# A decoder trunk step on one core: the first norm's and MLP norm's factors from one ones-matmul on all partitions, and the second result of a pooling group three channel blocks behind the first

## The chip, the cores and the metric

The kernel runs on one core of a Trainium2 chip. The time is that of one execution on the device in microseconds, from launch to end; before the change three runs gave 1097.31, 1097.84 and 1098.05, median 1097.84. A profiled execution gives the span (first to last instruction), what each engine did and what it waited for. The engines are PE (TensorE: matmuls), DVE (VectorE), ACT (ScalarE), POOL (GpSimd) and SP (SyncE, which issues the DMAs). Each works through its own instructions in a fixed order, and semaphores hold one back until what it needs is there.

## What is computed

One layer on 256 prompt tokens and 8 x 4 sample tokens, 288 in all. Cut to what matters:

```python
def rmsnorm(x, g):
    y = xf * lax.rsqrt(jnp.mean(xf * xf, axis=-1, keepdims=True) + EPS)
    return (y * g.astype(jnp.float32)).astype(x.dtype)

h = rmsnorm(x, norm1_g)                                  # D_MODEL = 2048
proj = jnp.einsum("btd,de->bte", h, w_in) + b_in
a, gate, z = proj[..., :D_CONV], proj[..., D_CONV:2 * D_CONV], proj[..., 2 * D_CONV:]
u = a * jax.nn.sigmoid(gate)                             # depthwise causal conv of 31 taps,
c = jax.nn.silu(layernorm(depthwise_causal_conv(u_ext, conv_w, conv_b), ln_g, ln_b))
d = multiscale_pool(z_ext, pos0)                         # windows 2, 4, 8, 16; four groups of 256
p = jnp.einsum("btgc,gce->btge", d, pool_w).reshape(bsz, T, D_POOL) * pool_scale
mix = jnp.concatenate([c, p], axis=-1)
x = x + jnp.einsum("btm,md->btd", mix, w_out)
h2 = rmsnorm(x, norm2_g)
f = jnp.square(jax.nn.relu(jnp.einsum("btd,df->btf", h2, w_ff1)))   # D_FF = 8192
x = x + jnp.einsum("btf,fd->btd", f, w_ff2)
```

A last rmsnorm and the new states of conv and pooling follow. All data are float32.

## The kernel before

**Layout.** Channels lie on the 128 partitions and the 288 tokens (T) along the free axis; x is sixteen blocks of 128x288 (`xT`). A float32 product is made of three matmuls: each operand is split into a rounded part and the rest (`hh` and `hl`, `whi` and `wlo`), and `product` (lines 253 to 255) issues hi x hi, hi x lo and lo x hi into one PSUM bank. So a result block of 128 channels over 16 channel blocks is 48 matmuls of 128x288.

**Weights.** They arrive in raw tiles of 512 KB (four channel blocks of two results). ACT writes `whi` (line 246); POOL, or later DVE, writes `wlo` (line 247). Each has four buffers, so the cast of a tile waits until PE has done with the tile four before it. `ready` holds the weights of the next `gemm`.

**Gemms.** `gemm` (line 257) makes two result blocks at a time, in the banks `bk[0]` and `bk[1]`: for each channel block k the product of result 0, then that of result 1. Both end together. There are four banks for such results (`ac`), so a gemm needs the banks of the last but one to have been read.

**Order of the work.** The first two conv groups run while x arrives; then, by `SEQUENCE`, conv groups 2 to 6, pool groups 3, 2 and 1, mix 3, pool group 0, mix 2 and conv group 7, then mix 1 and 0; then w_out in two halves of eight gemms (the first over the pool results, `mixp`, the second over the conv results, `mixc`), x1 with the squares for MLP norm beside the second half, and the MLP in four chunks of 16 gemms. The names `ac1`, `ac2`, ... number the banks in that order: ac11 and ac12 are conv group 6, ac13 and ac14 pool group 3, ac17 and ac18 pool group 1, ac19 and ac20 mix 3, ac21 and ac22 pool group 0, ac43 and ac44 the last gemm of w_out's first half, ac45 to ac48 the first two of its second half.

**What sets the order on an engine.** The tile framework's scheduler does, with a simulated timeline: it takes the program's priorities, the sizes and the buffers, and fixes each engine's list before the run. `later` (the conv taps) lowers a priority. A small edit can so move instructions far from it.

**The norms.** The rms factor isn't applied to the activations ahead of a gemm; each result is multiplied by it when its bank is read (`rb` in lines 368, 369 and 414, `r2` in line 544). The squares are summed over blocks first. `token_sum` (line 221) then sums over partitions: three matmuls with the tokens as rows and a column of ones give 96 partitions x 3 columns. `rsqrt_rows` (line 223) makes the factor of these: sqrt on ACT, five small DVE operations (with one Newton step), and three matmuls with the identity (line 238) that spread the row over all partitions (`pr`). For the first norm DVE copies that to `rb` (line 356); for MLP norm ACT copies it to `r2` (line 541). The layer norm of the conv part (`norm_begin`, `norm_end`, within w_out's first half) and the last norm use `rsqrt_rows` too.

**A pool group** (line 404): a gemm over all 16 blocks; then per result DVE multiplies by `rb` (line 414), ACT adds the bias and writes prompt and samples to `z_all` (lines 415 and 416), DVE sums the windows, and ACT and DVE split the outcome for the mix.

Of the kernel before, what the change touches and what calls it, by code (L numbers as in the profile page):

```python
# [9 lines left out]
F32 = mybir.dt.float32  # L10
# [6 lines left out]
P = 128  # L17
# [63 lines left out]
def trunk_kernel(ctx: ExitStack, tc: tile.TileContext, io):  # L81
# [15 lines left out]
    def nm(s):  # L97
        seen[s] = seen.get(s, 0) + 1
        return f"{s}{seen[s]}"
# [122 lines left out]

    def rsqrt_rows(pt, scale, after=None):

        st = const.tile([TB, 2, 3], F32, name=nm("st"))
        s1, s2 = st[:, 0, :], st[:, 1, :]
        p, h = pt[:TB, 0:3], pt[:TB, 4:7]
        nc.scalar.activation(s1, p, AF.Sqrt, bias=eps[:TB, 0:1], scale=scale)
        if after is not None:
            load_table(after, s1[:, 0:1])  # L230
        nc.vector.tensor_scalar(h, p, scale / 2, EPS / 2, op0=ALU.mult, op1=ALU.add)
        nc.vector.reciprocal(s2, s1)
        nc.vector.tensor_tensor(h, h, s2, op=ALU.mult)
        nc.vector.scalar_tensor_tensor(out=s2, in0=s1, scalar=0.5, in1=h, op0=ALU.mult, op1=ALU.add)
        nc.vector.reciprocal(s1, s2)
        pr = ms("pr")
        for j in range(3):
            nc.tensor.matmul(pr[:, j * TB : (j + 1) * TB], s1[:, j : j + 1].to_broadcast([TB, P]), ident, start=True, stop=True)  # L238
        return pr

    def split(raw, eng, cuts=((0, 4),)):

# [11 lines left out]
        nc.tensor.matmul(b, wh, xl, start=False, stop=False)  # L254
        nc.tensor.matmul(b, wl, xh, start=False, stop=last)  # L255

    def gemm(banks, rhs, m_outer=False, hooks={}):

        n = len(rhs)
        get = ready.pop()  # L260
        order = [(k, m) for k in range(n) for m in range(len(banks))]
        if m_outer:
            order.sort(key=lambda km: km[1])
        for j, (k, m) in enumerate(order):
            hooks.get(j, bool)()
            product(banks[m], rhs[k], get(k, m), k == 0, k == n - 1)
        ready.extend(itertools.islice(weights, 1))
# [36 lines left out]

    hx = []
    first_banks = bank2() + [bank("cv", cvp, "cv") for _ in range(2)]
    total = ms("total", 8)

    def square(c):

# [8 lines left out]
    for c in range(8):  # L319
        pair = []  # L320
        hi = wspl.tile([P, 4, 256], F32R, name=nm("whi"), tag="whi")
        lo = wspl.tile([P, 4, 256], F32R, name=nm("wlo"), tag="wlo")
        views = [t[:].rearrange("p (b k) n -> p b k n", b=2) for t in (first_raw[c], hi, lo)]
        steps = ((0, 1), (1, 2)) if c < 2 else ((0, 2),)
        for k0, k1 in steps:
            for k in range(2 * c + k0, 2 * c + k1):
                hh, hl = act("hh"), act("hl")
                nc.scalar.activation(hh, xT[:, k, :], AF.Copy, scale=v("norm1_g", k))  # L328
                nc.vector.scalar_tensor_tensor(out=hl, in0=xT[:, k, :], scalar=v("norm1_g", k), in1=f32(hh), op0=ALU.mult, op1=ALU.subtract)
                pair.append((hh, hl))  # L330
            if len(steps) == 2:
                r, h, l = [t[:, :, k0, :] for t in views]
            else:
                r, h, l = first_raw[c], hi, lo
            nc.scalar.copy(h, r)  # L335
            nc.vector.tensor_tensor(l, r, h.bitcast(F32) if len(steps) == 2 else f32(hi), op=ALU.subtract)
            for w, x in ((hi, 0), (hi, 1), (lo, 0)):
                if c == 7 and w is lo:
                    token_sum(total, rows[0])
                for k in range(k0, k1):  # L340
                    for m in range(4):
                        nc.tensor.matmul(  # L342
                            first_banks[m][:, :T], lhs(w, k, m), pair[k][x],
                            start=c == 0 and k == 0 and w is hi and x == 0, stop=c == 7 and k == 1 and w is lo,
                        )
                if c == 7 and w is hi and x == 0:
                    square(6)
                    square(7)
                    rows = [row("tot")]
                    nc.vector.tensor_tensor(rows[0], squares[:, 0, 0], squares[:, 0, 1], op=ALU.add)  # L350
        hx += pair
        if 0 < c < 7:
            square(c - 1)
    ready.extend(itertools.islice(weights, 1))
    rb = row("rb")
    nc.vector.tensor_copy(rb, rsqrt_rows(total, 1.0 / D, AF.Sigmoid)[:, :T])
    nc.gpsimd.memset(z_all[:, :, 0:PH], 0.0)

    cs = {}
# [44 lines left out]
    def pool_group(g):  # L404

        bk = bank2()
        gemm(bk, hx)
        w = WINDOWS[g]
        for m in range(2):
            i = 2 * g + m  # L410
            z = z_all[:, i, :]
            zs = samples(z[:, ZO:ZL], ZS)
            p = bk[m][:, :T]
            nc.vector.tensor_tensor(p, p, rb, op=ALU.mult)
            nc.scalar.activation(z[:, PH:ZO], p[:, 0:SEQ], AF.Identity, bias=v("b_in", 16 + i))
            nc.scalar.activation(zs[:, :, PH:ZS], samples(p[:, SEQ:T], NS), AF.Identity, bias=v("b_in", 16 + i))  # L416
            b = ms("d")[:, :T]
            s, step, n = z, 1, w
            if w > 8:
                s, step, n = tmp("s", ZL, "s", 2), 4, w // 4  # L420
                nc.vector.tensor_reduce(s[:, 3:ZL], windows(z[:, 0 : ZL - 3], (1, ZL - 3), (1, 4)), axis=AX.X, op=ALU.add)
            at = PH - step * (n - 1)
            nc.vector.tensor_reduce(b[:, 0:SEQ], windows(s[:, at:], (1, SEQ), (step, n)), axis=AX.X, op=ALU.add)
            nc.vector.tensor_reduce(samples(b[:, SEQ:T], NS), windows(s[:, ZO + at :], (ZS, NB), (1, NS), (step, n)), axis=AX.X, op=ALU.add)
            nc.vector.tensor_tensor(b[:, 0 : w - 1], b[:, 0 : w - 1], rise[:, g, 0 : w - 1], op=ALU.mult)
            nc.vector.scalar_tensor_tensor(out=b[:, 0:SEQ], in0=b[:, 0:SEQ], scalar=1.0 / w, in1=z[:, PH:ZO], op0=ALU.mult, op1=ALU.subtract)
            bs = samples(b[:, SEQ:T], NS)
            nc.vector.scalar_tensor_tensor(out=bs, in0=bs, scalar=1.0 / w, in1=zs[:, :, PH:], op0=ALU.mult, op1=ALU.subtract)
            dh, dl = act("dh", tag="p", bufs=16), act("dl", tag="p", bufs=16)
            nc.scalar.copy(dh, b)  # L430
            nc.vector.tensor_tensor(dl, b, f32(dh), op=ALU.subtract)
            dd[i] = (dh, dl)
# [96 lines left out]
                nc.vector.tensor_tensor(ss2, ss2, q2, op=ALU.add)  # L529

    r2 = row("r2")
    pss = ms("pss", 8)
    ssf = row("ssf")
    pf = ms("pf", 8)
    for ch in range(DFF // FCH):
        fx = []
        for g in range(FCH // 256):
            bk = bank2()
            gemm(bk, x1, hooks={4: lambda: token_sum(pss, ss2)} if ch == 0 and g == 0 else {})
            if ch == 0 and g == 0:  # L540
                nc.scalar.copy(r2, rsqrt_rows(pss, 1.0 / D)[:, :T])
            for m in range(2):
                t = tmp("t")
                nc.vector.scalar_tensor_tensor(out=t, in0=bk[m][:, :T], scalar=0.0, in1=r2, op0=ALU.max, op1=ALU.mult)
# [97 lines left out]
```

## Time and profile before

| | |
|---|---|
| median of three runs | 1097.84 us |
| the profiled execution: time, span | 1098.09 us, 1096.3 us |
| granted TensorE clock, mean | 0.995 |
| gemm matmuls of the MLP: mean of one | 0.29 to 0.30 us, overlapping |
| weight loads of PE (PEld) | 1081.0 us, beside the matmuls |
| DMA | 187.04 MB, mean 171 GB/s |
| POOL, DVE busy from 30 to 130 us | 95.82, 88.61 of 100 us |
| ACT casts of weights, L246 | 330, 1.051 us each |

Busy time is the union of the instructions on an engine; matmuls are pipelined, so one lasts longer than the step to the next, and the step is what counts. A row of the view in order of time has start, duration, engine, line, operation, output and inputs with their shape, the number of records ("x2") and in square brackets how long the engine stood idle ahead of it and what released it. Line numbers are those of the kernel printed above; the changed kernel's are 15 to 17 higher behind the new functions.

### The profile page before, as it was taken

Reading aid. Unit: us, or ns where it says so; the run is one execution under the profiler, and the core shown is the slowest. Engines: PE = TensorE matmul, PEld = TensorE weight load, DVE = VectorE, ACT = ScalarE, POOL = GpSimd, SP = SyncE. Lnnn points to the kernel's source line nnn. Section 1 sums busy time; section 2 is a strip of 40 time slices with the busy share of each in tenths; the row PEclk is TensorE's granted clock in tenths of the full one; section 3 lists DMA queues with packets and bytes.
Section 4 is the critical chain, followed back from the end, with each engine's and each line's share of the span. In section 5 each row is a group of like instructions: output and inputs, shape, how many; then the busy total and the mean of one; then the engine's idle time right before and its main releaser. Section 6 shows DMA issues by size and latency. Waiting matters only on the chain.

```text
span 1096.3 us, 19737 instructions
## 1 busy us (share of the span) xinstructions
PE 1082.3 (99%) x8186; PEld 1081.0 (99%) x8186; DVE 631.0 (58%) x982; ACT 471.8 (43%) x650; POOL 162.8 (15%) x108
## 2 busy tenths in 40 slices
PE   9999999999999999999999999999999999999995
PEld 9999999999999999999999999999999999999995
DVE  7798989687554544444554444555544445554553
ACT  7544454476444433334443333444433334444441
POOL 0899878500000000000000000000000000000000
PEclk9999999999999999999999999999999999999998
DMA  9655568555555555555555555555555555555522
GB/s 335 221 184 167 173 162 236 161 165 171 158 170 161 170 168 165 168 171 160 170 170 164 167 173 162 167 172 169 161 171 162 166 172 167 162 171 164 166 94 87
DMA packets 56649, 187.04 MB, mean 171 GB/s; under 512 B 5872, under 2 KB 11504, under 8 KB 56560
## 3 DMA queue, kind: packets, MB, share of 16 engines
q1 hardware_dynamic: 56416, 185.74, 54.3%
q8 instruction: 64, 1.05, 0.4%
q14 instruction: 25, 0.20, 0.1%
q10 hardware_dynamic: 144, 0.05, 0.0%
HBM read 181.49 MB, written 4.28 MB: 169 GB/s over the span
## 4 chain that ended last, share of the span: by engine, by line
PE 98%; DVE 1%; ACT 0%; DMA 0%; SPq 0%; issue 0%; DVEq 0%
PE ac L253 32%; PE ac L254 32%; PE ac L255 31%; PE ac L342 1%; PE cv L342 1%; DMA xT<-in_xT 0%; DVE xT L582 0%; PE pr L238 0%; ACT hh L328 0%; ACT uz L312 0%; PE pf L221 0%; ACT whi L335 0%; DVEq L628 0%; PE m L253 0%; PE m L254 0%
## 5 line engine op out<-in xcount | busy, mean ns | idle before, releaser
L246 ACT CAST whi<-wr 128x1024 fp32r<-128x1024 f32 x330 | 346.6, 1051 | 583.9 <-PE ac L254 553.7
L247 DVE TENSOR_TENSOR wlo<-wr,whi 128x1024 fp32r<-128x1024 f32 x272 | 333.3, 1225 | 373.7 <-ACT whi L246 373.7
L253 PE MATMUL ac<-ah,whi 128*128 128x288 f32 x1024 | 303.2, 296 | 0.0
L253 PE MATMUL ac<-fh,whi 128*128 128x288 f32 x1024 | 303.1, 296 | 0.0
L254 PE MATMUL ac<-fl,whi 128*128 128x288 f32 x1024 | 301.7, 295 | 0.0
L254 PE MATMUL ac<-al,whi 128*128 128x288 f32 x1024 | 301.6, 295 | 0.0
L255 PE MATMUL ac<-fh,wlo 128*128 128x288 f32 x1024 | 299.8, 293 | 0.0
L255 PE MATMUL ac<-ah,wlo 128*128 128x288 f32 x1024 | 299.4, 292 | 0.0
L255 PEld LDWEIGHTS ac<-fh,wlo 128*128 128x128 f32 x1024 | 193.5, 189 | 0.0
L255 PEld LDWEIGHTS ac<-ah,wlo 128*128 128x128 f32 x1024 | 193.4, 189 | 0.0
L254 PEld LDWEIGHTS ac<-fl,whi 128*128 128x128 f32 x1024 | 193.0, 188 | 0.0
L254 PEld LDWEIGHTS ac<-al,whi 128*128 128x128 f32 x1024 | 192.6, 188 | 0.0
L253 PEld LDWEIGHTS ac<-ah,whi 128*128 128x128 f32 x1024 | 192.4, 188 | 0.0
L253 PEld LDWEIGHTS ac<-fh,whi 128*128 128x128 f32 x1024 | 192.3, 188 | 0.0
L247 POOL TENSOR_TENSOR wlo<-wr,whi 128x1024 fp32r<-128x1024 f32 x58 | 138.6, 2414 | 25.2 <-ACT whi L246 23.0
L395 DVE SCALAR_TENSOR_TENSOR pc<-uz,vec,pc 128x256 f32<-128x256 f32 x232 | 98.7, 482 | 6.8 <-ACT pc L384 4.8
L253 PE MATMUL ac<-hh,whi 128*128 128x288 f32 x320 | 93.7, 296 | 0.7 <-ACT uz L416 0.7
L254 PE MATMUL ac<-hl,whi 128*128 128x288 f32 x320 | 93.8, 297 | 0.0
L255 PE MATMUL ac<-hh,wlo 128*128 128x288 f32 x320 | 88.5, 295 | 0.0
L253 PEld LDWEIGHTS ac<-hh,whi 128*128 128x128 f32 x320 | 60.3, 188 | 1.0 <-ACT uz L416 1.0
L254 PEld LDWEIGHTS ac<-hl,whi 128*128 128x128 f32 x320 | 60.4, 189 | 0.0
L255 PEld LDWEIGHTS ac<-hh,wlo 128*128 128x128 f32 x320 | 58.5, 189 | 0.0
(153 smaller groups left out, 878.2 us busy)
## 6 DMA issues: line engine op xcount, KB each, us to landing
wr<-in_w SPq DMA_DIRECT2D x336, 512.0 KB, 3.8
out_u_out<-uz SPq DMA_DIRECT2D x1, 1208.0 KB, 9.5
xT<-in_xT SPq DMA_DIRECT2D x2, 576.0 KB, 7.9
out_yT<-xT SPq DMA_DIRECT2D x2, 576.0 KB, 2.9
uz<-in_hist_c SPq DMA_DIRECT2D x1, 1088.0 KB, 11.8
wr<-in_w SPq DMA_DIRECT2D x4, 256.0 KB, 5.1
xT<-in_xT SPq DMA_DIRECT2D x3, 288.0 KB, 5.8
out_z_out<-uz SPq DMA_DIRECT2D x1, 668.0 KB, 9.8
```

The source lines that it names most:

```text
L246: nc.scalar.copy(hi[:, a:b, :], raw[:, a:b, :])
L247: eng.tensor_tensor(lo[:, a:b, :], raw[:, a:b, :], hi[:, a:b, :].bitcast(F32), op=ALU.subtract)
L253: nc.tensor.matmul(b, wh, xh, start=first, stop=False)
L254: nc.tensor.matmul(b, wh, xl, start=False, stop=False)
L255: nc.tensor.matmul(b, wl, xh, start=False, stop=last)
L342: nc.tensor.matmul(first_banks[m][:, :T], lhs(w, k, m), pair[k][x], start=c == 0 and k == 0 and w is hi and x == 0, stop=c == 7 and k == 1 ...
L395: nc.vector.scalar_tensor_tensor(out=dst, in0=u_all[:, i, w : w + SEQ], scalar=cw[i][:, w : w + 1], in1=pc[i], op0=ALU.mult, op1=ALU.add)
```

## The change

- First norm and MLP norm: `wide_sum` multiplies the 128x128 matrix of ones with the 128x288 squares, so that every partition holds every token's sum; `rsqrt_wide` does the steps of `rsqrt_rows` on 128x288 and writes `rb` or `r2` with its last reciprocal. The three narrow sums, the three spreading matmuls and the copy go.
- `gemm` takes a `lag`; the pool groups call it with 3. Products are sorted by k + 3m: result 0 begins with three blocks of its own, then they alternate, and result 1 ends with three blocks of its own.
- `rsqrt_rows` (still used by the conv part's norm and the last norm) writes its last reciprocal to a column of its own instead of over the sqrt.

```diff
@@ -222,8 +222,8 @@
 
     def rsqrt_rows(pt, scale, after=None):
 
-        st = const.tile([TB, 2, 3], F32, name=nm("st"))
-        s1, s2 = st[:, 0, :], st[:, 1, :]
+        st = const.tile([TB, 3, 3], F32, name=nm("st"))
+        s1, s2, y = st[:, 0, :], st[:, 1, :], st[:, 2, :]
         p, h = pt[:TB, 0:3], pt[:TB, 4:7]
         nc.scalar.activation(s1, p, AF.Sqrt, bias=eps[:TB, 0:1], scale=scale)
         if after is not None:
@@ -232,11 +232,28 @@
         nc.vector.reciprocal(s2, s1)
         nc.vector.tensor_tensor(h, h, s2, op=ALU.mult)
         nc.vector.scalar_tensor_tensor(out=s2, in0=s1, scalar=0.5, in1=h, op0=ALU.mult, op1=ALU.add)
-        nc.vector.reciprocal(s1, s2)
+        nc.vector.reciprocal(y, s2)
         pr = ms("pr")
         for j in range(3):
-            nc.tensor.matmul(pr[:, j * TB : (j + 1) * TB], s1[:, j : j + 1].to_broadcast([TB, P]), ident, start=True, stop=True)
+            nc.tensor.matmul(pr[:, j * TB : (j + 1) * TB], y[:, j : j + 1].to_broadcast([TB, P]), ident, start=True, stop=True)
         return pr
+
+    def wide_sum(bank, t):
+
+        nc.tensor.matmul(bank[:, :T], ones, t, start=True, stop=True)
+
+    def rsqrt_wide(bank, out, scale, after=None):
+
+        s1, s2 = tmp("s"), tmp("s")
+        b = bank[:, :T]
+        nc.scalar.activation(s1, b, AF.Sqrt, bias=eps[:, 0:1], scale=scale)
+        if after is not None:
+            load_table(after, s1[:, 0:1])
+        nc.vector.tensor_scalar(b, b, scale / 2, EPS / 2, op0=ALU.mult, op1=ALU.add)
+        nc.vector.reciprocal(s2, s1)
+        nc.vector.tensor_tensor(b, b, s2, op=ALU.mult)
+        nc.vector.scalar_tensor_tensor(out=s2, in0=s1, scalar=0.5, in1=b, op0=ALU.mult, op1=ALU.add)
+        nc.vector.reciprocal(out, s2)
 
     def split(raw, eng, cuts=((0, 4),)):
 
@@ -254,13 +271,13 @@
         nc.tensor.matmul(b, wh, xl, start=False, stop=False)
         nc.tensor.matmul(b, wl, xh, start=False, stop=last)
 
-    def gemm(banks, rhs, m_outer=False, hooks={}):
+    def gemm(banks, rhs, m_outer=False, hooks={}, lag=0):
 
         n = len(rhs)
         get = ready.pop()
         order = [(k, m) for k in range(n) for m in range(len(banks))]
-        if m_outer:
-            order.sort(key=lambda km: km[1])
+        if m_outer or lag:
+            order.sort(key=lambda km: km[1] if m_outer else km[0] + lag * km[1])
         for j, (k, m) in enumerate(order):
             hooks.get(j, bool)()
             product(banks[m], rhs[k], get(k, m), k == 0, k == n - 1)
@@ -304,7 +321,7 @@
 
     hx = []
     first_banks = bank2() + [bank("cv", cvp, "cv") for _ in range(2)]
-    total = ms("total", 8)
+    total = ms("total")
 
     def square(c):
 
@@ -336,7 +353,7 @@
             nc.vector.tensor_tensor(l, r, h.bitcast(F32) if len(steps) == 2 else f32(hi), op=ALU.subtract)
             for w, x in ((hi, 0), (hi, 1), (lo, 0)):
                 if c == 7 and w is lo:
-                    token_sum(total, rows[0])
+                    wide_sum(total, rows[0])
                 for k in range(k0, k1):
                     for m in range(4):
                         nc.tensor.matmul(
@@ -353,7 +370,7 @@
             square(c - 1)
     ready.extend(itertools.islice(weights, 1))
     rb = row("rb")
-    nc.vector.tensor_copy(rb, rsqrt_rows(total, 1.0 / D, AF.Sigmoid)[:, :T])
+    rsqrt_wide(total, rb, 1.0 / D, AF.Sigmoid)
     nc.gpsimd.memset(z_all[:, :, 0:PH], 0.0)
 
     cs = {}
@@ -404,7 +421,7 @@
     def pool_group(g):
 
         bk = bank2()
-        gemm(bk, hx)
+        gemm(bk, hx, lag=3)
         w = WINDOWS[g]
         for m in range(2):
             i = 2 * g + m
@@ -529,16 +546,16 @@
                 nc.vector.tensor_tensor(ss2, ss2, q2, op=ALU.add)
 
     r2 = row("r2")
-    pss = ms("pss", 8)
+    pss = ms("pss")
     ssf = row("ssf")
     pf = ms("pf", 8)
     for ch in range(DFF // FCH):
         fx = []
         for g in range(FCH // 256):
             bk = bank2()
-            gemm(bk, x1, hooks={4: lambda: token_sum(pss, ss2)} if ch == 0 and g == 0 else {})
+            gemm(bk, x1, hooks={4: lambda: wide_sum(pss, ss2)} if ch == 0 and g == 0 else {})
             if ch == 0 and g == 0:
-                nc.scalar.copy(r2, rsqrt_rows(pss, 1.0 / D)[:, :T])
+                rsqrt_wide(pss, r2, 1.0 / D)
             for m in range(2):
                 t = tmp("t")
                 nc.vector.scalar_tensor_tensor(out=t, in0=bk[m][:, :T], scalar=0.0, in1=r2, op0=ALU.max, op1=ALU.mult)
```

The edits move instructions elsewhere too. The lists below are each engine's instructions in program order (line, operation, output and inputs with the tiles' numbers, shape of the output; the second number in a name is internal).

ACT where pool group 1 (ac17 and ac18) and mix 3 (ac19 and ac20) end; `uz` is the state buffer that holds z, `ph` a split mix result, `dh` a split pooling result. Before:

```order
L443 ACTIVATE ph1_1917<-ac19_1879,vec_85 128x288
L415 ACTIVATE uz_87<-ac17_1743,vec_85 128x256
L416 ACTIVATE uz_87<-ac17_1743,vec_85 128x8x4
L443 ACTIVATE ph2_1921<-ac20_1880,vec_85 128x288
L415 ACTIVATE uz_87<-ac18_1744,vec_85 128x256
L416 ACTIVATE uz_87<-ac18_1744,vec_85 128x8x4
```

and now, where ac17's two instructions stand ahead of `ph1`:

```order
L263 CAST whi44_1895<-wr44_1889 128x1024
L432 ACTIVATE uz_87<-ac17_1737,vec_85 128x256
L433 ACTIVATE uz_87<-ac17_1737,vec_85 128x8x4
L460 ACTIVATE ph1_1911<-ac19_1873,vec_85 128x288
L460 ACTIVATE ph2_1915<-ac20_1874,vec_85 128x288
L432 ACTIVATE uz_87<-ac18_1738,vec_85 128x256
L433 ACTIVATE uz_87<-ac18_1738,vec_85 128x8x4
```

The reads of ac17 moved ahead of `ph1`, and the cast of whi44 is still the row before them.

PE around the end of pool group 3's predecessor: `ac11` and `ac12` are conv group 6, `ac13` is the first result of pool group 3. The last matmul on `whi25` and the first on `whi29`, which takes its buffer, now (the row with `hl4_231,whi25` is the last of its tile):

```order
L270 MATMUL ac12_1272<-hh4_230,whi25_1169 128x288
L271 MATMUL ac12_1272<-hl4_231,whi25_1169 128x288
L272 MATMUL ac12_1272<-hh4_230,wlo25_1170 128x288
L270 MATMUL ac11_1271<-hh5_251,whi26_1173 128x288
L271 MATMUL ac11_1271<-hl5_252,whi26_1173 128x288
L270 MATMUL ac12_1272<-hh5_251,whi26_1173 128x288
L271 MATMUL ac12_1272<-hl5_252,whi26_1173 128x288
L270 MATMUL ac13_1437<-hh1_174,whi29_1373 128x288
L271 MATMUL ac13_1437<-hl1_175,whi29_1373 128x288
L272 MATMUL ac11_1271<-hh5_251,wlo26_1174 128x288
L272 MATMUL ac12_1272<-hh5_251,wlo26_1174 128x288
```

Before, the same first matmul stood here, thirty rows behind the last one on `whi25`:

```order
L254 MATMUL ac12_1278<-hl9_328,whi27_1187 128x288
L253 MATMUL ac13_1443<-hh1_174,whi29_1379 128x288
L254 MATMUL ac13_1443<-hl1_175,whi29_1379 128x288
L253 MATMUL ac14_1444<-hh1_174,whi29_1379 128x288
L254 MATMUL ac14_1444<-hl1_175,whi29_1379 128x288
L255 MATMUL ac11_1277<-hh9_327,wlo27_1188 128x288
L255 MATMUL ac12_1278<-hh9_327,wlo27_1188 128x288
```

So the first two matmuls of pool group 3 have moved 24 rows forward, into conv group 6's second tile, and ac14's remain where tile 27 begins.

DVE where w_out's second half begins: `n` is a normalized conv block, `cc` its silu, `mh` and `ml` the split of it that the second half multiplies, and the additions to `xT` read the banks ac43 and ac44 of the first half's last gemm. Before:

```order
L492 TENSOR_TENSOR n1_2665<-c1_536,pr2_2661 128x288
L247 TENSOR_TENSOR wlo69_2977<-wr69_2972,whi69_2976 128x1024
L492 TENSOR_TENSOR n2_2673<-c2_539,pr2_2661 128x288
L497 TENSOR_TENSOR ml1_2668<-cc1_2669,mh1_2667 128x288
L492 TENSOR_TENSOR n3_2681<-c3_868,pr2_2661 128x288
L504 TENSOR_TENSOR xT_86<-xT_86,ac43_2857 128x288
L492 TENSOR_TENSOR n4_2689<-c4_871,pr2_2661 128x288
L504 TENSOR_TENSOR xT_86<-xT_86,ac44_2858 128x288
L497 TENSOR_TENSOR ml2_2676<-cc2_2677,mh2_2675 128x288
```

and now:

```order
L509 TENSOR_TENSOR n2_2667<-c2_533,pr1_2655 128x288
L509 TENSOR_TENSOR n3_2675<-c3_862,pr1_2655 128x288
L264 TENSOR_TENSOR wlo69_2971<-wr69_2966,whi69_2970 128x1024
L509 TENSOR_TENSOR n4_2683<-c4_865,pr1_2655 128x288
L521 TENSOR_TENSOR xT_86<-xT_86,ac43_2851 128x288
L509 TENSOR_TENSOR n5_2691<-c5_1195,pr1_2655 128x288
L514 TENSOR_TENSOR ml1_2662<-cc1_2663,mh1_2661 128x288
L521 TENSOR_TENSOR xT_86<-xT_86,ac44_2852 128x288
L509 TENSOR_TENSOR n6_2699<-c6_1198,pr1_2655 128x288
L264 TENSOR_TENSOR wlo70_2975<-wr70_2968,whi70_2974 128x1024
L514 TENSOR_TENSOR ml2_2670<-cc2_2671,mh2_2669 128x288
```

`ml1` came behind `n2` and ahead of ac43's addition; now it comes behind that addition and `n5`, and `ml2` behind the weight split `wlo70`. On ACT, likewise, `mh1` came behind the first `cc` and now comes behind the third, and the cast of whi70 ahead of `mh2`.

## The prediction

> **What bounds the kernel now.** I read the page first, then the list of what PE waits for, then the order in time around each place that the change touches.
>
> ```profile
> PE 1082.3 (99%) x8186; PEld 1081.0 (99%) x8186; DVE 631.0 (58%) x982; ACT 471.8 (43%) x650; POOL 162.8 (15%) x108
> PE 98%; DVE 1%; ACT 0%; DMA 0%; SPq 0%; issue 0%; DVEq 0%
> ```
>
> PE is busy for 99% of the span and holds 98% of the chain that ended last. So time is won in two ways only: fewer PE instructions, or fewer moments in which PE stands still. Inside the run there is one such moment:
>
> ```profile
> PE ac L253 <- ACT uz L416: 0.7, 1, 0.7
> ```
>
> The profiled execution took 1098.09 us, its span is 1096.3, so 1.8 lie around it; the median of the three timed runs, 1097.84, is 0.25 below it. The sum is made against 1098.09 and 0.25 is taken off at the end. A measurement of this kernel tells about 0.2%, 2.2 us, from no change.
>
> **Part 1: the two norms on PE.** In time order on PE (start, duration, line, operation); "x6" are six records of three matmuls:
>
> ```profile
> 27.59 0.59 PE L221 MATMUL total<-ones,tot 128*96 128x1 f32 x6
> 28.04 0.52 PE L342 MATMUL ac<-hl,whi 128*128 128x288 f32 x2
> 28.39 0.43 PE L342 MATMUL cv<-hl,whi 128*128 128x288 f32 x2
> ...
> 32.90 0.81 PE L238 MATMUL pr<-ident,st 96*128 96x96 f32 x6
> ...
> 33.70 0.30 PE L254 MATMUL ac<-hl,whi 128*128 128x288 f32 x1
> ...
> 278.75 0.59 PE L221 MATMUL pss<-ones,ss 128*96 128x1 f32 x6
> ...
> 279.42 0.29 PE L254 MATMUL ac<-al,whi 128*128 128x288 f32 x1
> ...
> 285.26 0.81 PE L238 MATMUL pr<-ident,st 96*128 96x96 f32 x6
> ...
> 286.07 0.30 PE L254 MATMUL ac<-al,whi 128*128 128x288 f32 x1
> ```
>
> Durations overlap, so I count starts. Gemm matmuls start 0.132 us apart (twelve starts, 135.78 to 137.24 below, are 11 steps in 1.46). The first token sum with two matmuls takes 28.39 - 27.59 = 0.80, of which two steps are the matmuls': it displaces 0.54. The first pr with one matmul takes 0.80: it displaces 0.67. For MLP norm it is 0.67 - 0.13 = 0.54 and 0.81 - 0.13 = 0.68. All four go: 2.43. What comes is two matmuls of a 128x128 f32 matrix by 128x288 f32. The kernel has that form once already, the mean of the conv groups:
>
> ```profile
> 201.47 0.65 PE L473 MATMUL pmean<-sum_c,avg 128*128 128x288 f32 x2
> 201.74 0.51 PE L255 MATMUL ac<-ph,wlo 128*128 128x288 f32 x1
> 202.09 0.29 PE L253 MATMUL ac<-ph,whi 128*128 128x288 f32 x1
> ```
>
> That is 202.09 - 201.47 - 0.13 = 0.49 each, 0.98 for both. **Part 1 gives 2.43 - 0.98 = 1.45 us less**, straight on the bound.
>
> **The rest of the norms.** Five DVE operations of 96x3 become five of 128x288, and a copy goes (DVE for the first norm, ACT for MLP norm).
>
> ```profile
> 33.74 0.46 DVE L356 COPY rb<-pr 128x288 f32<-128x288 f32 x1 [3.54 <-PE pr L238]
> ...
> 281.12 0.17 DVE L231 TENSOR_SCALAR pss<-pss 96x3 f32<-96x3 f32 x1 [0.35 <-ACT st L228]
> 281.19 0.16 DVE L232 RECIPROCAL st<-st 96x3 f32<-96x3 f32 x1
> ```
>
> A 128x288 operation takes 0.46. No row has a reciprocal that wide. At three elements it costs what a TENSOR_SCALAR does, so the near end is 0.46; a difference of 0.02 us would be seen there, which is 0.007 an element, so 0.46 + 288 x 0.007 = 2.5 us is an end that these rows bear; scaled by elements alone, 0.16 x 96 = 15 us, it is the far one. I take 0.46, since the 0.16 is a fixed cost by its neighbour: TENSOR_SCALAR's 0.17 scaled so would be 16 us as well, and a wide two-operand operation takes 0.46. [...]
>
> It hides behind PE: rb was ready at 33.74 + 0.46 = 34.2. With 2.5 a reciprocal, the chain from 28.1 is sqrt 0.5, three operations 1.4 and two reciprocals 5.0, so 35.0; DVE stood idle there (3.54 before the copy). PE first needs a bank that waits for rb 133 instructions behind the sum, 17.6 us, at about 45. For MLP norm it is 142 instructions, 18.7 us. Queued behind a slow reciprocal on DVE stand weight splits of L247, whose results are used some 70 matmuls (9 us) later. So: nothing. The reused st slot that rsqrt_rows gives up takes a wait from the group norm's last reciprocal, which lies ahead of an idle DVE: nothing either.
>
> **Part 2: pool groups.** The lag changes no instruction count; it moves when two results end and when two pairs of weight tiles are first and last used. Three places answer, and the queues.
>
> *Start of pool group 0 (the one stall).* PE, ACT and DVE in time order:
>
> ```profile
> 135.52 0.29 PE L254 MATMUL ac<-hl,whi 128*128 128x288 f32 x1
> ...
> 135.78 0.29 PE L253 MATMUL ac<-dh,whi 128*128 128x288 f32 x1
> ...
> 137.24 0.29 PE L255 MATMUL ac<-dh,wlo 128*128 128x288 f32 x1
> 138.28 0.40 PE L253 MATMUL ac<-hh,whi 128*128 128x288 f32 x1 [0.74 <-ACT uz L416]
> 138.51 0.30 PE L254 MATMUL ac<-hl,whi 128*128 128x288 f32 x1
> ```
> ```profile
> 135.90 1.05 ACT L246 CAST whi<-wr 128x1024 fp32r<-128x1024 f32 x1 [2.13 <-PE ac L254]
> 137.18 0.50 ACT L443 ACTIVATE ph<-ac,vec 128x288 fp32r<-128x288 f32 x1 [0.23 <-PE ac L255]
> 137.57 0.47 ACT L415 ACTIVATE uz<-ac,vec 128x256 f32<-128x256 f32 x1
> 137.93 0.29 ACT L416 ACTIVATE uz<-ac,vec 128x32 f32<-128x32 f32 x1
> ```
> ```profile
> 135.86 0.44 DVE L414 TENSOR_TENSOR ac<-ac,rb 128x288 f32<-128x288 f32 x1
> ```
>
> PE loses 138.28 - 137.24 - 0.13 = 0.91 and another 0.10 in a slow first step (0.23 for 0.13): 1.01. DVE was done with ac17 at 136.30; ACT read it only at 137.57, because the cast (held until 0.38 behind the start of a matmul on the old tile, 135.52) and the mix result ph1 stood ahead. Now L432 and L433 of ac17 stand ahead of ph1. With E the start of mix 3: cast from E + 0.12 to 1.17, L432 at 1.17, L433 from 1.53 (0.36 behind, as 137.57 to 137.93) to 1.82, PE on again 0.06 later, at 1.88, against 1.59 when its twelve matmuls are through. **0.30 + 0.10 stay of 1.01: 0.6 less**; the ends are 1.01 less and nothing.
>
> *Start of pool group 3.* The order shows that its first matmul, ac13 with whi29, was drawn forward into the end of conv group 6: it now stands six matmuls behind the last one that reads whi25, whose buffer the cast of whi29 takes; before it were thirty. By the rows above a cast starts 0.38 behind the start of the matmul that frees its buffer, takes 1.05 and lets PE go 0.06 later: 1.49, against 6 x 0.132 = 0.79. Before, thirty matmuls (4.0 us) covered it. **A new stall, 0.70 + 0.10: 0.8 more.** Ends: nothing (if something else had set that cast's time) and 1.3 (if the 0.5 us activation ahead of it is late as well).
>
> *Queues.* SP's transfers keep their order; on POOL one split trades places with an L388 product in the first conv groups and near 160 us a sum of L400 goes ahead of one split. A split of the weights on POOL takes 2.41 us:
>
> ```profile
> L247 POOL TENSOR_TENSOR wlo<-wr,whi 128x1024 fp32r<-128x1024 f32 x58 | 138.6, 2414 | 25.2 <-ACT whi L246 23.0
> ```
>
> Two splits are first used 24 matmuls, 3.2 us, apart, so with a sum of some 0.8 between them the second is still in time: nothing.
>
> *Start of w_out's second half.* The scheduler has also reordered DVE and ACT where the first conv result meets w_out:
>
> ```profile
> 217.51 0.81 PE L238 MATMUL pr<-ident,st 96*128 96x96 f32 x6
> ...
> 221.20 0.43 PE L253 MATMUL ac<-mh,whi 128*128 128x288 f32 x2
> 221.47 0.30 PE L254 MATMUL ac<-ml,whi 128*128 128x288 f32 x1
> ```
> ```profile
> 218.73 1.22 DVE L247 TENSOR_TENSOR wlo<-wr,whi 128x1024 fp32r<-128x1024 f32 x1
> ...
> 220.23 0.45 DVE L497 TENSOR_TENSOR ml<-cc,mh 128x288 fp32r<-128x288 f32 x1
> ...
> 221.01 0.45 DVE L504 TENSOR_TENSOR xT<-xT,ac 128x288 f32<-128x288 f32 x1
> ```
> ```profile
> 218.84 0.63 ACT L495 ACTIVATE cc<-n,vec 128x288 f32<-128x288 f32 x1 [0.31 <-DVE n L492]
> 219.50 0.43 ACT L496 CAST mh<-cc 128x288 fp32r<-128x288 f32 x1
> ```
>
> Before, ml1 was done at 220.68 and PE took it at 221.47, 0.8 us to spare. Now ml1 stands behind the x addition of ac43 and n5 on DVE. That addition waits for a matmul four ahead of the second half's first (G): released at G - 0.53 + 0.38 = G - 0.15, then n5 and ml1 one step of 0.37 each behind it, ml1 from G + 0.59 to 1.04, PE on at 1.10. The three first matmuls that need only mh1 last to G + 0.5 (the third waits 0.1 for the addition): a hole of 0.6. Twelve matmuls later it wants ml2, which now stands behind ac44's addition, n6 and a weight split of 1.13: done at G + 3.27, wanted at about G + 2.9: 0.4. With slow first steps of 0.10 each: **about 1.25 more**. The ends are nothing (as before) and 2.0 (two more DVE steps of 0.37 ahead of ml1).
>
> **Sum:** -1.45 - 0.6 + 0.8 + 1.25 = 0.0. So 1098.1 on the profiled scale, **1097.8 us** on that of the median: the gain is real, and is given back.
>
> **The rivals.**
> - *Only one of the two new stalls forms:* -0.8 or -1.25, so 1097.0 or 1096.6. For it: both rest on times worked out, not seen. 0.14.
> - *Neither forms:* 1097.84 - 1.45 - 0.6 = 1095.8, and 1095.4 if pool group 0's stall goes too. For it: the same two places held in the profile of before, and DVE and ACT are 58% and 43% busy. Against it: an engine's order is fixed, and a matmul six places behind the release of a 1.05 us cast can't be fed in 0.79. 0.16.
> - *The lag leaves pool 0's stall as it is*, since something else releases it: 0.6 more, 1098.4. 0.05.
> - *The wide reciprocal becomes the bound, and it is slower than before.* Place: DVE, between the sqrt and the first use of the factor. The point where two reciprocals outlast the cover is, in the first norm, (17.6 - 0.5 - 1.9 and the four evictions ahead of the bank, 1.5, so 13.7) / 2 = 6.9 us each; behind that each microsecond counts twice. At 8 us it is 2.3 there and, with the MLP norm's 1 us more of cover, 1.2 there: +3.5, 1101.3; at the far end of 15 us some 30 more. Against it: the 0.16 beside 0.17. 0.06.
> - *The TensorE clock falls in the stalls.* At the program's start eight matmuls took 6.97 - 4.92 = 2.05 us, twice the usual step; a stall in w_out's second half followed by 3.8 us at that half speed would cost 1.9, two of them 3.8: 1101.6. The row behind the 0.91 us stall of before has a granted clock of 1.00 (seventh figure, ahead of the DMA share). [...] 0.02.
>
> ```profile
> 4.92 0.83 PE L342 MATMUL ac<-hh,whi 128*128 128x288 f32 x2
> ...
> 6.97 0.42 PE L342 MATMUL ac<-hh,wlo 128*128 128x288 f32 x2
> ```
> ```profile
> 138.20:142.00 3.80, 3.72 (x27) 3.73 (x28) 3.80 (x13) 1.36 (x6) 1.21 (x1) 1.00 0.64 201
> ```
>
> **How the numbers follow.** The forecast has 0.57. It, the single stall and the unchanged pool 0 lie within 0.2% (0.76); so does a third of "neither" (0.05): same 0.81. Two thirds of "neither", with pool 0's stall gone as well or part 1 a little better, fall below 1095.65: faster 0.11. The last two make slower 0.08. The bounds of the terms give -1.45 - 1.01 = -2.5 and -1.45 + 1.3 + 2.0 = +1.9, so 1095.4 to 1099.7; the slower two stay outside.
>
> **What would show it.** PE's waits in the changed profile should list ACT whi under the gemm (0.7, at pool group 3's start), DVE ml (two, 1.0 together), and ACT uz at 0.3 in place of 0.7; the two sums should displace 0.49 each and nothing of pr be left but the group norm's and the last norm's. rb's reciprocal should end before 36 us. Were the ACT whi and DVE ml waits missing, the gain of 2 us would stand and I am wrong on the low side; a wait for rb or r2 in PE's list would be the reciprocal.

## The result, and the profile after

The changed kernel takes 1103.51 us (median of 6 runs, 1102.94 to 1104.51) against 1097.41 for the kernel before beside it (6 runs, 1096.82 to 1098.05): a ratio of 1.0053, 95% interval 1.0043 to 1.0063. It is slower, and outside the predicted range. The profiled span is 1101.9 us against 1096.3.

The page of the changed kernel: busy time by engine, and the chain that ended last.

```profile
PE 1086.6 (99%) x8166; PEld 1084.3 (98%) x8166; DVE 639.6 (58%) x981; ACT 472.0 (43%) x649; POOL 162.9 (15%) x108
```
```profile
PE 98%; DVE 1%; DMA 0%; ACT 0%; SPq 0%; issue 0%; DVEq 0%; ACTq 0%
```

PE has 20 instructions fewer and is busy for 4.3 us longer. What it waited for (total, times, longest, in us):

```profile
PE ac L359 <- ACT whi L352: 1.5, 2, 1.3
PE pr L238 <- DVE st L235: 1.2, 1, 1.2
PE warm L209 <- DVE ones L195: 1.1, 1, 1.1
PE pf L221 <- ACT q L582: 1.0, 1, 1.0
PE ac L271 <- DVE ml L514: 0.6, 2, 0.3
PE ac L270 <- ACT whi L263: 0.5, 1, 0.5
```

The last two rows are the new stalls, at w_out's second half (DVE ml, two of them) and at pool group 3 (ACT whi); the wait for uz has sunk out of the list. The first is in the loop over the arriving input, at the program's start. It was 0.4 before and lies between 0.2 and 1.6 in the kernels below; the first norm's sum starts between 27.2 and 28.1 us in all of them, against 27.59 before, so less than half a microsecond comes of it. The predicted places, in time order on PE in the changed kernel:

```profile
27.66 0.65 PE L243 MATMUL total<-tot,ones 128*128 128x288 f32 x2
27.93 0.65 PE L359 MATMUL ac<-hl,whi 128*128 128x288 f32 x2
28.41 0.29 PE L359 MATMUL cv<-hl,whi 128*128 128x288 f32 x1
...
87.75 0.30 PE L271 MATMUL ac<-hl,whi 128*128 128x288 f32 x1
88.57 0.40 PE L270 MATMUL ac<-hh,whi 128*128 128x288 f32 x1 [0.52 <-ACT whi L263]
88.81 0.29 PE L271 MATMUL ac<-hl,whi 128*128 128x288 f32 x1
...
137.61 0.29 PE L272 MATMUL ac<-dh,wlo 128*128 128x288 f32 x1
137.91 0.40 PE L270 MATMUL ac<-hh,whi 128*128 128x288 f32 x1
138.15 0.29 PE L271 MATMUL ac<-hl,whi 128*128 128x288 f32 x1
...
220.81 0.71 PE L270 MATMUL ac<-mh,whi 128*128 128x288 f32 x3
221.85 0.40 PE L271 MATMUL ac<-ml,whi 128*128 128x288 f32 x1 [0.33 <-DVE ml L514]
222.09 0.29 PE L272 MATMUL ac<-mh,wlo 128*128 128x288 f32 x1
...
223.15 0.69 PE L270 MATMUL ac<-mh,whi 128*128 128x288 f32 x4
224.09 0.40 PE L271 MATMUL ac<-ml,whi 128*128 128x288 f32 x1 [0.24 <-DVE ml L514]
224.32 0.29 PE L272 MATMUL ac<-mh,wlo 128*128 128x288 f32 x1
...
279.56 0.65 PE L243 MATMUL pss<-ss,ones 128*128 128x288 f32 x2
279.83 0.51 PE L270 MATMUL ac<-ah,whi 128*128 128x288 f32 x1
280.17 0.29 PE L271 MATMUL ac<-al,whi 128*128 128x288 f32 x1
```

Read by starts, less 0.13 us for each matmul that belongs there: the sums displace 0.49 and 0.48; pool group 3 stalls for 0.69 and a slow first step of 0.11; pool group 0 for 0.17 and 0.11 (1.01 before); w_out's second half for 0.64 + 0.11 and 0.41 + 0.10. Beside the prediction's terms:

```
term                       predicted   measured
both norms on PE             -1.45       -1.46
pool group 0's stall         -0.6        -0.73
pool group 3's new stall     +0.8        +0.80
w_out's two new stalls       +1.25       +1.26
sum                           0.0        -0.13
span                          0.0        +5.6
```

Every term of the sum came out, and 5.7 us came from somewhere else. Two pairs of rows show where: the MLP norm's sum pss (quoted above and in the prediction), and the program's last token sum (before, then after).

```profile
1083.49 0.67 PE L221 MATMUL pf<-ones,q 128*96 128x1 f32 x6 [1.02 <-ACT q L565]
```
```profile
1089.07 0.67 PE L221 MATMUL pf<-ones,q 128*96 128x1 f32 x6 [1.02 <-ACT q L582]
```

Up to pss the changed kernel takes 279.56 - 278.75 = 0.81 more, where the terms ahead of it give 0.6 (-0.72 for the first norm, -0.73 + 0.80 + 1.26). From pss to pf it takes 809.51 against 804.74: 4.77 more, where the list of its instructions holds 0.74 less (the MLP norm's own part). So **the MLP is 5.5 us slower on an unchanged list**: but for the norm's own, the same 6144 matmuls in the same order. It isn't a stall: the only row of PE's waits that lies there is the 1.02 ahead of pf, in both. Eight gemms in the middle of the MLP, 768 matmuls from the first on x1's first block to the first on fx, before and after:

```profile
475.74 0.30 PE L253 MATMUL ac<-ah,whi 128*128 128x288 f32 x1
...
576.70 0.30 PE L253 MATMUL ac<-fh,whi 128*128 128x288 f32 x1
```
```profile
476.82 0.30 PE L270 MATMUL ac<-ah,whi 128*128 128x288 f32 x1
...
578.58 0.30 PE L270 MATMUL ac<-fh,whi 128*128 128x288 f32 x1
```

100.96 us are 131.5 ns a matmul, 101.76 are 132.5. Cut into eighths of 768 matmuls, and without the first and the last, which hold the norm's sum and that of the last norm, the MLP runs at 131.4 to 131.9 before and at 132.5 after. 6144 matmuls at 0.9 ns are 5.5 us. Neither the clock (seventh figure) nor the DMA (eighth and ninth: share, GB/s) differs between the two (windows view, before and after):

```profile
500.00:600.00 100.00, 100.00 (x763) 100.00 (x762) 50.22 (x63) 42.98 (x60) 0.00 (x0) 1.00 0.54 166
```
```profile
500.00:600.00 100.00, 100.00 (x757) 100.00 (x756) 51.20 (x62) 42.10 (x60) 0.00 (x0) 1.00 0.53 167
```

The start times of successive matmuls show what differs: both kernels repeat a pattern of steps, and not the same one. From the 19th gemm of the MLP, in ns (the changed kernel, and the same kernel with one more matmul, the last experiment below, which steps much as the kernel before does):

```
changed kernel         137 126 132 133 133 132 | 138 126 131 134 132 133 | 137 126 132 133 132 133
with one more matmul   133 130 126 131 134 132 131 132 131 | 133 130 126 131 134 132 131 132 131
```

The steps repeat with a period of six, at a mean of 132.2, against a period of nine, at 131.1. The last quarter of that gemm follows another pattern in both, with some longer steps; with it the means are 132.5 and 131.4. I call them the slow and the fast rhythm.

### The profile page after: what moved, and what is told of

It is laid out like the page before. It is cut to its first block, busy times and chain, and to the rows that moved or that the text cites. A ratio compares the mean times of both kernels' runs of the same rounds, so it can differ in the third digit from the quotient of the medians.

```text
span 1101.9 us, 19685 instructions
## 1 busy us (share of the span) xinstructions
PE 1086.6 (99%) x8166; PEld 1084.3 (98%) x8166; DVE 639.6 (58%) x981; ACT 472.0 (43%) x649; POOL 162.9 (15%) x108
## 4 chain that ended last, share of the span: by engine, by line
PE 98%; DVE 1%; DMA 0%; ACT 0%; SPq 0%; issue 0%; DVEq 0%; ACTq 0%
PE ac L270 32%; PE ac L272 32%; PE ac L271 32%; PE ac L359 1%; PE cv L359 1%; DMA xT<-in_xT 0%; DVE xT L599 0%; PE pr L238 0%; DVE wlo L264 0%; PE pf L221 0%; ACT whi L263 0%; ACT hh L345 0%; SPq L171 0%; SPq L164 0%; DVE n L509 0%
```

## The experiments

Times are medians beside the kernel before on the same chip, ratios have their 95% intervals. "MLP" is from the start of pss to the start of the pf group behind q, "ahead" is what lies before; ns is the step over the eight gemms above.

**Which part of the change?** Each part was put into the kernel before by itself, and the changed kernel was run without the lag. In question were (A) the buffers, which take turns in another order in the MLP when something ahead of it has moved, (B) a rhythm of PE that the MLP norm's small matmuls shift, (C) the pool groups' order with the lag. The diffs are cut to the added lines that matter; `wide_sum` and `rsqrt_wide` are those of the change, and `rsqrt_rows` keeps its old slot wherever a part stands alone.

First norm alone:

```diff
+    total = ms("total")
+                    wide_sum(total, rows[0])
+    rsqrt_wide(total, rb, 1.0 / D, AF.Sigmoid)
```


> Only the first norm is made wide; MLP norm, the pool groups and the st slot are as before. The profile of the change shows that its extra time lies in the MLP: 131.4 to 132.0 ns from one matmul to the next before, 132.5 after, over 6144 matmuls (5.5 us), on the same list of instructions. Theory A: the buffers decide (this kernel's weight tiles and PSUM banks take turns as in the changed kernel), so the MLP runs at 132.5 ns here too and the time is 1103.5. Theory B: a rhythm of PE that the small matmuls of MLP norm's old form shift early in the MLP (they are still here), so 131.4 to 132.0 ns and 1098.0. Both: the stalls at pool group 3's start (0.7) and w_out's second half (0.6 and 0.4) are here as well, since this kernel's lists have them too.

MLP norm alone:

```diff
+    pss = ms("pss")
+            gemm(bk, x1, hooks={4: lambda: wide_sum(pss, ss2)} if ch == 0 and g == 0 else {})
+                rsqrt_wide(pss, r2, 1.0 / D)
```


> Only MLP norm is made wide; the rest is as before. The buffers take turns as before. Theory A (the buffers decide): the MLP at 131.4 to 132.0 ns a step, 1096.7 us. Theory B (the removed small matmuls decide): 132.5 ns, 1102.2 us. Both: no new stall, since the lists of pool group 3 and of w_out's second half are as before.

Lag alone:

```diff
+        if m_outer or lag:
+            order.sort(key=lambda km: km[1] if m_outer else km[0] + lag * km[1])
+        gemm(bk, hx, lag=3)
```


> Only the lag of 3 in the pool groups; both norms and the st slot as before. Its buffers take turns as in the changed kernel, its first matmul of pool group 3 stands 30 behind (as before), its w_out second half has the changed order. Theory A: the MLP at 132.5 ns, 1103.4 us. Theory B: 131.4 to 132.0 ns, 1097.9 us. Both: the stall of pool group 0 shrinks to 0.2 to 0.3, no stall at pool group 3, 0.6 and 0.4 at w_out's second half.

The changed kernel without the lag:

```diff
-        gemm(bk, hx, lag=3)
+        gemm(bk, hx)
```


> Both norms wide and the st slot, without the lag. Theories A and B: the MLP at 132.5 ns, 1102.7 us. If the lag were needed for the slow MLP (theory C: it is the pool groups' own order that does it), 131.4 to 132.0 ns and 1097.2 us. The stalls are those of the changed kernel in all cases, by the order of the lists.

And the MLP norm and the lag without the first norm (the diffs of the second and third together, the old slot too):

> MLP norm wide and the lag, the first norm as before. Its lists have the changed order at w_out's second half (stalls of 0.6 and 0.4) and pool group 0 (0.3 in place of 1.0), not at pool group 3. By the sum 1097.4 - 0.7 - 0.7 + 1.2 = 1097.2 us with the MLP at 131.4 to 132.0 ns, 1102.5 us with it at 132.5. If what comes ahead of the MLP (the w_out part of the list) sets the rhythm, it is 132.5 as in the three other kernels with that part; if MLP norm's form sets it, 131.4 to 132.0 as in the kernel with MLP norm alone.

```
in the kernel                      us       ratio                     ahead    MLP      ns
nothing (before)                                                     278.75   804.74   131.5
first norm                       1104.35   1.0059 [1.0044, 1.0074]   279.75   810.23   132.5
MLP norm                         1097.06   0.9992 [0.9983, 1.0002]   278.65   803.87   131.5
lag                              1103.41   1.0050 [1.0033, 1.0067]   279.04   810.24   132.5
both norms                       1103.17   1.0050 [1.0035, 1.0065]   279.47   809.51   132.5
MLP norm and lag                 1096.80   0.9992 [0.9983, 1.0001]   278.98   803.67   131.4
all three (the change)           1103.51   1.0053 [1.0043, 1.0063]   279.56   809.51   132.5
```

MLP takes one of two values, some 804 to 805 or 810 us, and what the kernels do in it differs by some 0.7 only. The first norm alone brings the slow one, the lag alone too, the MLP norm doesn't: as theory A had it in the first four, where B and C each missed. But the lag with the MLP norm is fast. So the lag has no price of its own in the MLP, and it adds nothing to the two norms (the last row against that of both); nor does the MLP norm's form decide, since the changed kernel has it and is slow. The first norm is in slow kernels each time in this table; that it can be fast as well, the last experiment shows.

These runs also say where the moves ahead of the MLP come from. PE's waits in the kernel with the first norm alone, and in the one with the lag alone:

```profile
PE ac L271 <- DVE ml L514: 0.6, 2, 0.3
PE ac L270 <- ACT whi L263: 0.5, 1, 0.5
```
```profile
PE ac L254 <- DVE ml L497: 0.6, 2, 0.3
```

The first norm alone has the new stalls at both places (and pool group 0's has shrunk to 0.18); the lag alone has w_out's and no stall at pool group 3.

**Is it which buffer is read when?** Behind the MLP norm the lists of both kernels are the same but for the buffers, which take turns in another order: the two banks of a gemm's results (2, 1 and 3, 0 where they were 2, 3 and 0, 1), and the four buffers each of whi (2 3 1 0 for 3 2 1 0) and wlo (2 1 3 0). Fixed turns for the banks:

```diff
+    turn = itertools.count()
-        return [bank("ac") for _ in range(2)]
+        return [acc.tile([P, 512], F32, name=nm("ac"), tag=f"ac{(0, 1, 2, 3)[next(turn) % 4]}", bufs=1) for _ in range(2)]
```


> The changed kernel with the four result banks taken in a fixed turn, so a gemm has banks 0 and 1 or 2 and 3 (in the changed kernel it has 2 and 1 or 3 and 0; before the change 2 and 3 or 0 and 1). The weight tiles take turns as in the changed kernel (whi buffers 2 3 1 0, wlo 2 1 3 0). Theory A1, the pairs of banks decide: the MLP at 131.4 to 132.0 ns a step and 1098.0 us. Theories A2 and A3 (below): 132.5 ns and 1103.5 us.

1105.53, 1.0070 [1.0055, 1.0085], MLP 809.50, 132.5 ns: A1 fails. The fixed turn also brought a new stall of 1.6 us ahead of the MLP, up to 153.7 us.

The turn of the weights can be changed by one matmul that reads a weight tile again, late enough to hold its buffer past its turn; the result goes to a bank that nobody reads. In the diffs, cut to the place from here on, the numbers in braces count from 0: the gemm (or chunk and gemm), and the product ahead of which the matmul stands; `once_more(k, part)` reads the tile of channel block k, part 0 being whi and 1 wlo:

```diff
+    def once_more(k, part):
+        spare = ms("spare")
+        nc.tensor.matmul(spare[:, :T], keep[0](k, 0)[part], x1[0][0], start=True, stop=True)
...
+ {3: {24: lambda: once_more(4, 0)}}.get(g, {}) if ch == 0 else {}
```


> The changed kernel with one matmul more, without a use for its result, in the fourth gemm of the MLP: it reads a whi tile once more behind the last use of the next tile, so that two whi buffers come free in the other order and take turns 2 1 3 0 from there on, as wlo does; no other instruction moves. Theory A2, what decides is whether whi and wlo take turns in the same order: 131.4 to 132.0 ns from the sixth MLP gemm on, 1098.6 us. Theory A1 (banks) and A3 (whi's turn in descending order, 3 2 1 0): 132.5 ns and 1103.7 us.

1098.19, 1.0003 [0.9994, 1.0013], MLP 804.12, 131.4 ns from the next gemm on. Taken by itself, that speaks for the turns, as theory A2 has it. The next two put whi alone, and then both, to the turn of the kernel before:

```diff
+ {3: {16: lambda: once_more(0, 0)}}
```


> As the run with whi's turn like wlo's, but the extra matmul stands eight products earlier, so that whi takes turns 3 2 1 0 (its order before the change) and wlo stays at 2 1 3 0. Theory A3: 131.4 to 132.0 ns, 1098.6 us. Theory A2: 132.5 ns or slower, since the orders still differ, 1103.7 us. Theory A1: 132.5 ns, 1103.7 us.

```diff
+ {3: {16: lambda: once_more(0, 0), 24: lambda: once_more(4, 1)}, 4: {16: lambda: once_more(0, 1)}}
```


> Three extra matmuls in the fourth and fifth MLP gemm, so that whi and wlo both take turns 3 2 1 0 from there, as before the change; banks as in the changed kernel. Theories A2 and A3: 131.4 to 132.0 ns, 1098.9 us. Theory A1: 132.5 ns, 1104.0 us.

1103.50, 1.0052 [1.0037, 1.0067], and 1104.04, 1.0055 [1.0038, 1.0072]; both 132.5 ns. With the weights' turns those of before the MLP is still slow, so A2 and A3 fail. Two theories were left: M, that the whole assignment of buffers decides, and L, that it tells nothing and that small disturbances put PE into one rhythm or the other. Two runs bear on M: all turns, banks too, as before in the changed kernel, and the kernel before with one whi turn changed by such a matmul.

```diff
+ {3: {16: lambda: once_more(0, 0), 24: lambda: once_more(4, 1)}, 4: {16: lambda: once_more(0, 1)}}
+        return [acc.tile([P, 512], F32, name=nm("ac"), tag=f"ac{(0, 1, 2, 3)[next(turn) % 4]}", bufs=1) for _ in range(2)]
```


> The changed kernel with whi and wlo both at turns 3 2 1 0 from the fifth MLP gemm on and the banks in order (0 and 1, 2 and 3): all of the assignment of before the change. Theory M: 131.4 to 132.0 ns from there on; with the 1.8 us stall that the fixed banks alone brought near 152 us, 1100.7 us. Theory L: the assignment tells nothing; 132.5 ns as in the run with both orders descending (1105.9 us) or 131.4 to 132.0.

```diff
+ {3: {24: lambda: once_more(4, 0)}}
```


> The kernel before the change with the one extra matmul of the run that gave whi wlo's turn, at the same place; here it makes the turns differ (whi 3 1 2 0, wlo 3 2 1 0). Theory M as far as it says that differing turns are slow: 132.5 ns from the sixth MLP gemm on, 1102.8 us. Theory L: the turns tell nothing; the extra matmul alone does or doesn't disturb the rhythm (1097.9 or 1102.8), and it then does the same in the run with the eleven at this first place.

1105.79, 1.0074 [1.0059, 1.0089], 132.5 ns; and 1098.03, 1.0003 [0.9994, 1.0013], 131.5 ns. M misses both. The buffers of before don't bring its pace, and another turn doesn't take it away. Two kernels of the table above show the same from the other side: in the programs as built, the one with the first norm alone and the one with MLP norm and lag read and write the same addresses in each of the MLP's matmuls behind the norm's sum, and the first is slow, the second fast.

**Is it the disturbance itself?** Extra matmuls that read a tile still in use, so that no turn moves, at places spread over the MLP, in the changed kernel and in the kernel before. Of eleven places two name a product beyond the gemm's 32 and add nothing.

```diff
+ {(0, 3): {24: lambda: once_more(12, 0)}, (0, 6): {8: lambda: once_more(4, 0)}, (1, 1): {16: lambda: once_more(8, 0)}, ...
```


> The changed kernel with eleven single matmuls more in the MLP, without a use for their results, at different places of its gemms (two or three in each quarter of the MLP, two gemms apart); each reads a tile that is in use anyway, so that no buffer's turn and no other instruction moves. The runs so far leave two theories. Theory M: the whole assignment of buffers decides (whi, wlo and banks together; no one of them alone). Then the MLP stays at 132.5 ns a step between all eleven, 1105 us. Theory L: on one list and one assignment PE has two rhythms, each of which keeps itself up, and small disturbances decide which one it falls into. Then some of the eleven turn 132.5 into 131.4 to 132.0 ns until the next, or back; 1100 to 1105 us.

> The kernel before the change with the same eleven matmuls at the same places. Theory M: 131.4 to 132.0 ns throughout, 1099 us. Theory L: some of the eleven turn that into 132.5 ns until the next; 1099 to 1104 us.

The first: 1101.60, 1.0036 [1.0023, 1.0049]. Its steps, from the starts of each gemm (a gemm's place is its number in the MLP, and how many products of it come first):

```
gemms 1 to 3                              132.5 ns
matmul added in gemm 4, product 24     -> 131.4
                     7,          8     -> 132.5
                    18,         16     -> 132.5 (stays)
                    20,         24     -> 131.4
                    34,         12     -> 131.4 (stays)
                    36,         24     -> 132.5
                    38,          4     -> 132.5 (stays)
                    50,         20     -> 132.5 (stays)
                    54,         30     -> 131.4 to the end
```

One matmul switches the pace in either direction, or leaves it, and the pace then holds until a later one switches it. Of the six that met the slow pace three switched it. M had it slow throughout. The second: 1099.55, 1.0017 [1.0008, 1.0027]; there the pace is back at 131.4 to 132.0 within two gemms of each, so none made the kernel before slow, where theory L had expected some to. Then a single one of them, the first, in the changed kernel:

```diff
+ {(0, 3): {24: lambda: once_more(12, 0)}}.get((ch, g), {})
```


> The changed kernel with one single matmul more in its fourth MLP gemm, ahead of the 25th product, reading a tile in use: no buffer's turn and no other instruction moves. Theory L (two rhythms): the MLP goes from 132.5 to 131.4 to 132.0 ns there and stays so to its end, 1098.3 us, 5 us less than the changed kernel for 0.1 us more of work. Theory M (assignment): 132.5 ns to the end, 1103.7 us. Were it to fall back at the next quarter of the MLP, 1101 to 1102 us and the rhythm would need a refresh.

1098.19, 1.0004 [0.9995, 1.0013], MLP 804.13: as theory L had it. The run with whi's turn like wlo's had its matmul at the same place, and the same MLP time within 0.01 us, with other turns. In time order on PE, with the matmul that is added, and the rows that begin and end the eight gemms:

```profile
320.65 0.29 PE L271 MATMUL ac<-al,whi 128*128 128x288 f32 x1
320.78 0.30 PE L272 MATMUL ac<-ah,wlo 128*128 128x288 f32 x1
320.91 0.30 PE L327 MATMUL spare<-ah,whi 128*128 128x288 f32 x1
321.05 0.29 PE L270 MATMUL ac<-ah,whi 128*128 128x288 f32 x1
...
476.03 0.30 PE L270 MATMUL ac<-ah,whi 128*128 128x288 f32 x1
...
576.94 0.29 PE L270 MATMUL ac<-fh,whi 128*128 128x288 f32 x1
```

100.91 us, 131.4 ns. A matmul whose result nobody reads, and which takes 0.13 us, makes the changed kernel 5.3 us faster (it stands 0.4 us above the kernel before on the same chip, where the change stood 6.1 above). That is what was not foreseen, all but 0.4 us of it.

## Why the prediction was wrong

**The step that failed** is the first: "So time is won in two ways only: fewer PE instructions, or fewer moments in which PE stands still". It took the 0.132 us from one matmul to the next for a constant, read off eleven steps at one place. There is a third way: the step itself. It went from 131.4 to 131.9 ns up to 132.5 in the MLP, and 6144 of them weigh more than all terms of the sum. That it isn't one constant could be seen in the profile of before: its MLP steps by 131.4 to 131.9 where those eleven steps gave 132.7. The range was drawn from the bounds of the terms, so it couldn't hold this; the 0.08 for slower was given to two mechanisms that didn't act.

**The terms** were right in sign and place, and nearly in size: only pool group 0's stall ended 0.1 us better than foreseen. In the fast rhythm, with one matmul more, the changed kernel takes 1098.19 where 1097.8 was predicted.

**Where they come from** was wrong. The stalls at pool group 3 and in w_out, and the gain at pool group 0, were set down under the lag; the first norm alone brings all three, and the lag alone has no stall at pool group 3. The MLP norm alone has none of these: PE's wait for uz is 0.7 there as before. The sum came out all the same, since its terms were read off the lists of the whole change.

**The reciprocal** was taken at 0.46 us, with 2.5 as an end. It takes 1.95 (DVE in time order, the first norm, then what follows it):

```profile
29.25 1.94 DVE L253 RECIPROCAL s<-s 128x288 f32<-128x288 f32 x1
...
32.22 1.95 DVE L256 RECIPROCAL rb<-s 128x288 f32<-128x288 f32 x1
34.28 0.47 DVE L385 TENSOR_TENSOR cv<-cv,rb 128x288 f32<-128x288 f32 x1
```

That the three-element one costs what its neighbour does said little of a wide one. The end of 2.5, worked out from what the rows at three elements could leave unseen, lies nearer to it than the 0.46 that I chose. It cost nothing: rb is there at 34.17, as before, PE's list has no wait for rb or r2, and so that rival did not come true.

**The clock** didn't fall either. The stretch from ahead of w_out's first stall into the second, and that with the second and what follows, have a granted clock of 1.00:

```profile
220.50:224.00 3.50, 3.01 (x20) 2.47 (x18) 3.38 (x8) 3.50 (x8) 0.00 (x0) 1.00 0.49 154
222.00:226.00 4.00, 3.75 (x27) 3.52 (x28) 4.00 (x10) 3.74 (x10) 0.00 (x0) 1.00 0.49 165
```

The steps say the same: behind the slow first step that follows each of these two stalls, of 0.64 and 0.41 us, matmuls start 0.13 us apart (from 222.09 to 223.15 are 8 steps, from 224.32 to the row below 12).

```profile
225.91 0.29 PE L272 MATMUL ac<-mh,wlo 128*128 128x288 f32 x1
```

So the 3.8 us at half speed by which I priced this rival were my estimate; this profile shows no such stretch. Nor is it shown that the clock made the doubled steps at the program's start, from which that half speed was read: the granted clock is 1.00 there too (before).

```profile
5.00:8.00 3.00, 2.66 (x14) 2.43 (x12) 0.96 (x2) 1.59 (x4) 0.00 (x0) 1.00 0.98 338
```

**What stays open.** What inside PE makes two rhythms of one list, and why a given disturbance ends in the one or the other. The kernel with MLP norm and lag and the changed kernel step alike to 1 ns over the 358 steps ahead of the wide sum of the MLP norm, on the same list and with the buffers in the same turn, and part at the second gemm matmul behind it (steps of 126 and 133 ns). What of the little in which they differ decides that is not shown. Nor is a version shown to beat the kernel before: the MLP norm alone, and with the lag, stand at 0.9992, with intervals that reach past 1.

## What to carry to other kernels

Where PE is busy for 99%, count the same number of matmuls between two rows that both traces have, and compare the step, before a difference is put down to an edit. If the step differs on an unchanged list, add one harmless matmul, at several places, since only three of six switched the slow pace here: if one flips it, the price is not the edit's, and a change that looks 0.5% worse (or better) may be neither. A forecast for such a kernel needs this as a case of its own, beside its terms.

## What the hardware showed that was not expected

- The same list of matmuls runs at 131.4 to 131.9 or at 132.5 ns a matmul at a granted clock of 1.00, and keeps to it for hundreds of microseconds (in the changed kernel for the six middle eighths of the MLP, 4608 matmuls or some 610 us); one matmul more can switch it. Which one it is, is a matter of the kernel and not of the run: the changed kernel's six runs lie between 1102.94 and 1104.51 us, the eleven with one matmul more, as in the last experiment, between 1097.45 and 1098.74.
- A reciprocal of 128x288 takes 1.95 us, where a sum or product of that size takes 0.46; at 96x3 both take 0.15 to 0.17.
- After each of the stalls shown PE's first step is 0.10 to 0.11 us longer.
